# Attention value products on 64x64 tiles, upper and lower key halves in separate PSUM banks, in a hybrid encoder layer on one Trainium2 core

## The chip, the cores and the metric

The kernel runs on one core of a Trainium2 chip. The metric is the device time in microseconds (us). The engines are TensorE (PE in the profile, its weight loads PEld), VectorE (DVE), ScalarE (ACT), GpSimd (POOL) and SyncE (SP, which issues DMAs). SBUF is the on-chip memory, with 128 partitions; PSUM holds the results of matmuls, in banks of 128 partitions by 512 f32 numbers.

## The reference

One encoder layer with two parallel paths, over 4096 tokens of width 1024. The attention path has 8 query heads of 64 and 2 key-value heads, and a window of 128 tokens to each side, computed in blocks of 128 queries against 384 keys.

```python
o = jnp.einsum('bnkgqs,bnskd->bnqkgd', p.astype(v.dtype), vw)   # p: softmax with a sink, zero outside the window
...
a = banded_attention(q, k, v, rel_bias, attn_sink[l]) * jax.nn.silu(g_a)
p = multiscale_pool(u_p, pool_w[l], pool_scale[l]) * jax.nn.silu(g_p)
mixed = jnp.einsum('bse,ed->bsd', jnp.concatenate([a, p], axis=-1), w_out[l])
x = x + rmsnorm(mixed, post_norm_g[l])
```

The change concerns the first line, the product of attention weights and values, and the multiplication of its result by `silu(g_a)`, the gate.

## The kernel before

The program has two parts. Up to about 510 us it projects the gates and the pooled path and stores their results in DRAM. From there to the end it computes queries, keys and values, attention and the output product. Numbers are carried as pairs of f16 (a high part and the rest, "low"), so a product of two such numbers is three matmuls: high by high, low by high, high by low.

The second part goes through 32 blocks of 128 queries, from block 31 down to block 0. Two blocks are a unit `u`. For each block and each half of the head groups the steps are:

- `scores` (PE): queries by keys, on 64x32 tiles, into the score banks `s`.
- `logits` (DVE, L1336), four instructions: add the bias, take the maximum, write `p` to SBUF. The last one frees the score bank.
- `exps` (ACT, L1347), `denominators` (DVE), `probs` (ACT, L1369, the high part of the weights) and `rests` (DVE, L1377, the low part).
- `turn`: a DMA that transposes the weights into `pt`.
- `values` (PE, L1482), once for both halves: the value products. `vv` are the values, with keys on the partitions; the result has values on the partitions and queries along the free axis.
- `gate` (DVE, L1506): the result times the scale `gaf` and the gate `ga` (called `gb` in the trace), into `at`, 128x512 f32.

`gate` is followed by the output product in a form that saves matmuls: the four quarters of a pair of blocks are combined by sums (`sum1` L1567, `sum3` L1570 and `sum2` L1573 on DVE, `sum4` L1576 on POOL), each sum is cast to its high part (`high`, ACT L1534) and its low part (`low`, POOL or DVE L1538), and `product` (PE, L1632) multiplies each of the quarters and sums (named "11", "12", "22", "s1" to "s4") by a part of the output weights. `begin` (ACT L1650), `gain11` (DVE L1660), `gain` (L1666), `add` (DVE L1671) and `square` (ACT L1655) gather these products and norms from the PSUM banks `acc0`, `acc1` and `acc2`, and so free them. The same three banks hold the query, key and value projections (`aq`, `kv`, PE L1273 and L1414, kept by `keep_q` and the like with ACT L1262 and DVE L1263) and one half of the value products. The other half has a bank `o` of its own, with one buffer.

A block has the keys of three neighbouring blocks `kb` = 0, 1, 2. Besides `kb` 1, queries 0 to 63 of a block (`LOW`) see all of `kb` 0 and the lower half of `kb` 2; queries 64 to 127 (`TOP`) see all of `kb` 2 and the upper half of `kb` 0. Before, `LOW` queries accumulate in bank `o` and `TOP` queries in bank `p` (one of `acc`). Whole key blocks are taken with 128 keys on the partitions, as matmuls of 128x64 weights by 128 columns (two head groups in two column halves of the array). The edge halves (`kb` 2 for `LOW`, `kb` 0 for `TOP`) follow at the end on 64x64 tiles. An inner block has 72 matmuls and 72 weight loads. `gate` is two DVE instructions, one on each bank, each with half of the queries of all heads (128x256).

The order of all instructions is written out by hand: `due(t, fn, ...)` puts a step into a plan with a time, `pe(...)` does it for PE steps one behind the other, `at_` for steps at a time from a stretch's start `z`, `cast` for a pair of `high` and `low`, `soft` for a softmax. The plan is sorted by these times and each engine issues in that order; the engine then waits by semaphores. The head (blocks 31 to 28) and the tail (2 to 0) are tables of `at_` times. Between them a loop goes over the blocks from 27 down to 2, an odd and an even visit in one iteration of two blocks: an odd visit of block b has the value products and the gate of block b + 1 (even) and then `sums`; an even visit those of the odd block, and two query projections.

Of the kernel before, what the change touches and what calls it, by code (L numbers as in the profile page):

```python
# [8 lines left out]
F32 = mybir.dt.float32  # L9
# [3 lines left out]
AF = mybir.ActivationFunctionType  # L13
ALU = mybir.AluOpType
# [3 lines left out]
P = 128  # L18
# [5 lines left out]
NB = S // P  # L24
# [110 lines left out]
def hybrid_layer(ctx: ExitStack, tc, io, out):  # L135
    nc = tc.nc
# [25 lines left out]
    gaf = const.tile([P, 1], F32, name="gaf")  # L162
# [48 lines left out]
    with ExitStack() as actx:  # L211
# [13 lines left out]
        rows = pa.tile([P, T], F32, name="rows")  # L225
# [9 lines left out]
        def turn(name):  # L235
            turns[name] += 1
            return turns[name] % 2
# [377 lines left out]
        def pair(q, op, i, scale, key, group):  # L615
            src, r, w = raws[q][:, i], quarter_keys(q, i), f"w{slot[q, op]}"
            do("ACT", act(D) + 0.1, key, w_high, q, op, src, scale, r=r + [f"sw{group}"],
               w=[f"{w}h"])
            do("DVE", dve(D), key + 0.1, w_low, q, op, src, scale,
               r=r + [f"sw{group}", f"{w}h"], w=[f"{w}l"])  # L620
# [333 lines left out]
        b = turn("n2")  # L954
        for j in range(4):
            ld(9.5 + 0.1 * j, wut[:, j], io["w_uT"][j], 0.5, w=[f"wut{j}"])
            z = turn("sq")
            for half in range(2):
                t = U0 + 4 * j + 2 * half
# [245 lines left out]
        g = 0  # L1205
# [29 lines left out]
    pb = ctx.enter_context(tc.tile_pool(name="pb", bufs=2, reuse_waits="tile"))  # L1235
# [15 lines left out]
    q_t, v_t = {}, {}  # L1251
# [27 lines left out]
    pt, p_t, nm_t, den_t, rd_t, pn_t = {}, {}, {}, {}, {}, {}  # L1279

    def keys(b):
        return [kb for kb in range(3) if 0 <= b - 1 + kb < NB]
# [6 lines left out]
    def due(t, fn, *args):  # L1289
        plan.append((t, len(plan), fn, args))  # L1290
# [168 lines left out]
    ga_t, o_t = {}, {}  # L1459
# [5 lines left out]
    def values(b, bank):  # L1465
        kbs = keys(b)
        if bank is None:
            other = s_t[1][:, 0]
        else:
            other = gemm.tile([P, 512], F32, name=f"p{b}", tag=f"acc{bank}")  # L1470
        o_t[b] = [
            t[:, : 2 * P].rearrange("p (h j q) -> p h j q", h=2, j=2)
            for t in (ps_o.tile([P, 512], F32, name=f"o{b}", tag="o"), other)
        ]
        terms = ((0, 0), (1, 0), (0, 1))
        LOW, TOP = slice(0, P // 2), slice(P // 2, P)

        def part(half, kb, ks, side, vi, pi, start=False, stop=False):
            ku, kt = divmod(b - 1 + kb, 2)
            for g in range(2):  # L1480
                a = slice(64 * g, 64 * g + 64)
                nc.tensor.matmul(  # L1482
                    o_t[b][side][a, half], v_t[ku][ks, vi, kt, a],
                    pt[b, half][ks, pi, g, :, kb - kbs[0], (LOW, TOP)[side]],
                    start=start, stop=stop, skip_group_check=True,
                )

        for half in range(2):
            for kb, sides in ((1, (0, 1)), (0, (0,)), (2, (1,))):
                if kb in kbs:  # L1490
                    for n, (vi, pi) in enumerate(terms):
                        for side in sides:
                            part(half, kb, slice(0, P), side, vi, pi, start=(half == 0 and kb == 1 and n == 0))
        for half in range(2):
            for n, (vi, pi) in enumerate(terms):
                if 2 in kbs:
                    part(half, 2, LOW, 0, vi, pi, stop=(n == 2))
                if 0 in kbs:
                    part(half, 0, TOP, 1, vi, pi, stop=(n == 2))

    def gate(b):
        at[b] = pb.tile([P, 4, P], F32, name=f"at{b}", tag="at")
        o, ga = o_t.pop(b), ga_t.pop(b)
        for side in range(2):
            qs = slice(64 * side, 64 * side + 64)
            nc.vector.scalar_tensor_tensor(  # L1506
                out=at[b][:, :, qs], in0=o[side].rearrange("p h j q -> p (h j) q"), scalar=gaf,
                in1=ga[:, :, qs], op0=ALU.mult, op1=ALU.mult,
            )

    at, yf, y_t, mo_t, z_t, ss_t, xr_t, rs_t = {}, {}, {}, {}, {}, {}, {}, {}

# [63 lines left out]
    def sums(u, t):  # L1578
        due(t, sum1, u)
        due(t + 0.05, sum3, u)  # L1580
        due(t + 0.1, sum2, u)
        pair(t + 1.1, u, "s2", a11)
        pair(t + 10.0, u, "s3", a21)
        pair(t + 10.6, u, "s1", a_s1)
        due(t + 5.0, sum4, u)
        pair(t + 11.3, u, "s4", a12)
# [125 lines left out]
    def pe(us, fn, *args):  # L1712

        due(now[0], fn, *args)
        now[0] += us
        return now[0]
# [20 lines left out]

    def attend(b, bank):
        t = pe(2.0, values, b, bank)
        due(t, gate, b)  # L1740
        if b % 2:
            pair(t + 0.8, b // 2, "11", a11)
        else:
            sums(b // 2, t + 0.7)
# [51 lines left out]
    def at_(t, fn, *args):  # L1796
        due(z + t, fn, *args)
# [11 lines left out]
    def cast(th, tw, u, name, f, eng):  # L1809
        at_(th, high, u, name, f)  # L1810
        at_(tw, low, u, name, f, eng)
# [9 lines left out]
    for t, fn, *args in (  # L1821
# [13 lines left out]
        (32.6, scores, NB - 2, 1),  # L1835
        (33.7, proj_q1, U - 1, 1, 1, 1),
        (36.4, values, NB - 1, 0),
        (38.4, product, U, "22", OT4, 2),
        (41.0, scores, NB - 3, 0),
        (42.0, proj_k, U - 2, 1),  # L1840
        (44.7, proj_v, U - 2),
        (47.5, scores, NB - 3, 1),
        (48.4, product, U, "11", O11, 0),
        (51.1, values, NB - 2, 1),
        (53.1, product, U, "12", O21, 0, True),
        (55.7, scores, NB - 4, 0),
# [27 lines left out]
    cast(26.2, 27.0, U, "12", a12, G)  # L1874
    at_(33.9, keep_q, U - 1, 0)
    at_(38.35, keep_q, U - 1, 1)
    at_(38.37, gate, NB - 1)
    cast(41.0, 41.6, U, "11", a11, G)
    at_(46.3, keep_k, U - 2)
    at_(47.2, keep_v, U - 2)  # L1880
    at_(50.5, begin, U)
    at_(53.1, gate, NB - 2)
    at_(53.2, sum1, U)
    at_(54.1, sum3, U)
# [6 lines left out]
    at_(62.0, low_q, U - 2, 0)  # L1891
    at_(64.75, add, U, (0, HI), (0, HI), 0)
    cast(66.2, 66.8, U, "s3", a21, G)
    at_(66.75, gate, NB - 3)
    cast(66.8, 67.4, U, "s1", a_s1, G)
    cast(67.4, 68.0, U, "s4", a12, G)
# [35 lines left out]
    for b in reversed(range(2, NB - 4)):  # L1932
# [7 lines left out]
        if b % 2:  # L1940
            mix_p3(u + 2)
            do_kv(u - 1)
            attend(b + 1, int(b == NB - 5))
            visit(b, 1)
            mix_p4(u + 1)
            mix_p1(u + 1)
            mix_p6(u + 1)
            mix_p2(u + 1)
        else:
            do_q(u - 1, 0)  # L1950
            attend(b + 1, 0)
            visit(b, 1)
            do_q(u - 1, 1)
            due(now[0] + 2.1, load_x, u - 3)
            if b > 2:
                mix_p7(u + 1)
                mix_p5(u + 1)
# [54 lines left out]
    cast(5.8, 6.4, 1, "22", a22, G)  # L2012
    cast(6.4, 10.2, 1, "12", a12, G)
    at_(9.0, begin, 1)
    at_(13.7, gate, 2)
    at_(14.4, sum1, 1)
    at_(15.1, sum3, 1)
# [21 lines left out]

    cast(24.7, 26.1, 0, "22", a22, G)  # L2040
    cast(34.35, 35.0, 0, "12", a12, G)
    at_(33.9, gate, 1)
    cast(37.6, 38.6, 0, "11", a11, V)
    at_(45.9, gate, 0)
    cast(46.7, 47.3, 0, "21", a21, V)
    at_(30.0, open_unit, 0)
# [97 lines left out]
```

## Time and profile before

| | |
|---|---|
| median of 3 runs | 1164.87 us (1164.27 to 1165.51) |
| the profiled execution's own time | 1164.42 us |
| its span, first to last instruction | 1162.6 us |
| granted TensorE clock, mean | 1.000 |
| ACT busy | 701.7 us (60%), 1460 instructions |
| POOL busy | 314.4 us (27%), 310 instructions |

The profile shows one execution. "Busy" is the time in which an engine executes at least one instruction; register, branch, semaphore and DMA-issuing instructions don't count. A row of a timeline has the start in us from the span's start, the duration, the engine, the line of the kernel, the operation, output and inputs by name, the shape and a count; a bracket tells how long the engine was idle before it, and who ended this idle time. The timeline rolls neighbouring rows of one kind into one with a count. Ends of matmuls are modelled, so differences between starts are the better measure on PE.

### The profile page before, as it was taken

To read this page: it belongs to the slowest core of one execution; us is meant where nothing else is said; L and a number is where in the kernel's file an instruction comes from. 1 tells how busy PE (TensorE), PEld (TensorE's weight loads), DVE (VectorE), ACT (ScalarE), POOL (GpSimd) and SP (SyncE) were. 2 spreads that over 40 slices of the span, in tenths; PEclk is the share of its full clock that TensorE was granted. 3 is DMA by queue.
4 is the path that set the end of the run, shared out by engine and by line. 5 is a ranking of instruction groups with operands and counts; after the bars stand their busy time and mean duration, and the time that the engine had idled before them with its cause. 6 is when DMAs were issued, how large, how long until landed. Compare 5 with 4: busy or idle time off the path is not lost. (4 is left out here: it accounts for less than half of the span.)

```text
span 1162.6 us, 33001 instructions
## 1 busy us (share of the span) xinstructions
PE 1145.9 (99%) x13804; PEld 879.4 (76%) x13804; DVE 937.7 (81%) x1875; ACT 701.7 (60%) x1460; POOL 314.4 (27%) x310
## 2 busy tenths in 40 slices
PE   7999999999999999999999999999999999999997
PEld 6998888888888888986667676676666767667653
DVE  6889988988799973568878877887887887787786
ACT  6876546546654542267676676666666666666672
POOL 0001121211111010201534433533442443353231
PEclk9999999999999999999999999999999999999999
DMA  9645585867667664299886776886787678686784
GB/s 340 220 127 181 173 272 176 283 222 246 218 191 232 210 169 133 85 279 242 233 202 136 196 200 139 193 205 179 156 191 193 136 204 201 133 198 157 173 214 145
DMA packets 292981, 226.30 MB, mean 195 GB/s; under 512 B 210864, under 2 KB 250800, under 8 KB 288224
## 3 DMA queue, kind: packets, MB, share of 16 engines
q1 hardware_dynamic: 292832, 224.20, 69.8%
q8 instruction: 108, 1.77, 0.6%
q14 instruction: 41, 0.34, 0.1%
HBM read 114.68 MB, written 60.34 MB: 151 GB/s over the span
## 5 line engine op out<-in xcount | busy, mean ns | idle before, releaser
L689 PEld LDWEIGHTS <-wq 128*128 128x128 f16 x4104 | 400.9, 98 | 52.0 <-DVE wq L310 2.9
L689 PE MATMUL y<-xt,wq 128*128 128x256 f16 x1512 | 203.3, 273 | 0.1
L1347 ACT ACTIVATE p<-p,nm 128x385 f32<-128x385 f32 (+1 forms) x256 | 152.8, 599 | 36.5 <-POOL p L1330 20.4
L1273 PE MATMUL aq<-xb,xb 128*128 128x256 f16 x1024 | 173.4, 273 | 0.4 <-DVE mo L1671 0.4
L1632 PE MATMUL ms<-wo,ys 128*128 128x512 f16 x720 | 162.8, 379 | 0.3 <-DVE mo L1671 0.3
L1377 DVE SCALAR_TENSOR_TENSOR pn<-p,rd,pn 128x384 f16<-128x384 f32 (+1 forms) x256 | 158.3, 669 | 5.9 <-ACT pn L1369 5.9
L1336 DVE CUSTOM_DVE_ANT_0 p<-s,nt,nsink 128x384 f32<-128x384 f32 (+1 forms) x256 | 155.9, 666 | 2.0 <-PE s L1313 2.0
L1273 PEld LDWEIGHTS <-xb 128*128 128x128 f16 x1280 | 125.1, 98 | 23.4 <-issue 7.8
L1273 PE MATMUL aq<-xb,xt 128*128 128x256 f16 x512 | 139.6, 273 | 0.0
L1369 ACT ACTIVATE pn<-p,rd 128x384 f16<-128x384 f32 (+1 forms) x256 | 134.5, 596 | 4.0 <-issue 1.1
L307 POOL TENSOR_TENSOR yt<-yt,sg 128x512 f32<-128x512 f32 (+2 forms) x32 | 51.0, 1595 | 301.6 <-DVE yt L310 232.3
L1632 PEld LDWEIGHTS <-ys 128*128 128x128 f16 x720 | 69.2, 98 | 82.2 <-issue 3.8
L1632 PE MATMUL m<-wo,y 128*128 128x512 f16 x540 | 121.8, 379 | 0.0
L1632 PEld LDWEIGHTS <-y 128*128 128x128 f16 x540 | 51.4, 98 | 63.5 <-issue 3.6
L1666 POOL TENSOR_TENSOR mo<-mo,gpost 128x512 f32<-128x512 f32 x39 | 63.8, 1636 | 93.8 <-ACT jkb L1655 92.6
L689 PE MATMUL plain<-xb,wq 128*128 128x256 f16 x576 | 67.0, 273 | 3.7 <-DVE wq L310 2.3
L1273 PEld LDWEIGHTS <-xt 128*128 128x128 f16 x640 | 62.6, 98 | 8.7 <-issue 0.4
L689 PE MATMUL v<-xt,wq 128*128 128x256 f16 x504 | 68.6, 273 | 0.1
L689 PE MATMUL y<-xb,wq 128*128 128x256 f16 x504 | 68.6, 273 | 0.0
L689 PE MATMUL v<-xb,wq 128*128 128x256 f16 x504 | 68.6, 273 | 0.0
L689 PE MATMUL x<-xb,wq 128*128 128x256 f16 x504 | 68.1, 273 | 0.5 <-DVE ubuf L310 0.5
L1538 POOL TENSOR_TENSOR ys<-at,ys 128x512 f16<-128x512 f32 x29 | 38.5, 1326 | 93.3 <-ACT ys L1534 93.3
(218 smaller groups left out, 1935.4 us busy)
## 6 DMA issues: line engine op xcount, KB each, us to landing
nt<-in_xT SPq DMA_DIRECT2D x28, 512.0 KB
x_scr<-xb SPq DMA_DIRECT2D x14, 1024.0 KB
xb<-x_scr SPq DMA_DIRECT2D x14, 1024.0 KB
xr<-in_x SPq DMA_DIRECT2D x28, 512.0 KB
out<-xr SPq DMA_DIRECT2D x28, 512.0 KB
xn<-in_x SPq DMA_DIRECT2D x27, 512.0 KB
ga_scr<-cc SPq DMA_DIRECT2D x64, 128.0 KB
raw<-in_w_out SPq DMA_DIRECT2D x16, 512.0 KB
```

What stands on the lines that cost most here:

```text
L307: eng.tensor_tensor(out=out, in0=in0, in1=in1, op=op)
L689: nc.tensor.matmul(b[:, s], wq[:, slot[q, op], wv, s, k, :], x[:, xv, k, :], start=(first and k + s + wv + xv == 0), stop=(last and k == H ...
L1273: nc.tensor.matmul(acc, w[:, j, k, :], x[:, kh, v, kt, :], start=(n == 0), stop=(n == 3 * KT - 1),)
L1336: nc.vector.tensor_tensor_reduce(out=p_t[b, half][:, hh, :nk], in0=s_t[jj][:, gg, :nk], in1=bias[:, h, lo : lo + nk], scale=negc[:, h : h ...
L1347: nc.scalar.activation(p[:, hh, : nk + 1], p[:, hh, : nk + 1], AF.Exp, bias=nm_t[b, half][:, hh : hh + 1], scale=-1.0, accum_out=den_t[b, ...
L1369: nc.scalar.activation(prob_view(b, half)[:, 0, i], p_t[b, half][:, i, :nk], AF.Copy, scale=rd_t[b, half][:, i : i + 1],)
L1377: nc.vector.scalar_tensor_tensor(out=pn4[:, 1, i], in0=p_t[b, half][:, i, :nk], scalar=rd_t[b, half][:, i : i + 1], in1=pn4[:, 0, i], op0= ...
L1538: eng.tensor_tensor(out=y[:, :, 1], in0=f(u), in1=y[:, :, 0], op=ALU.subtract)
L1632: nc.tensor.matmul(z_t[u, tag], y[:, k, yi, :], wo[o][:, wi, k, :], start=(n == 0 and acc is None), stop=(n == 3 * HK - 1), skip_group_che ...
L1666: eng.tensor_tensor(out=mo, in0=mo, in1=gpost[:, cs], op=ALU.mult)
```

## The change

All value products use 64x64 tiles now. Each key block is cut into rows 0 to 63 and rows 64 to 127; the lower rows accumulate in bank `o`, the upper rows in bank `p`, each for all queries of the block (256 columns: two heads by 128 queries). Where the window cuts a half key block off (`kb` 0 with lower rows, `kb` 2 with upper rows), only the 64 queries that see it are taken (128 columns). A block still has 72 matmuls and 72 weight loads. As each bank now holds a part of the sum for all queries, the banks have to be added: a new step `copy_o` on ACT copies bank `o`, scaled, to `at`; `gate` is a DVE instruction that adds the scaled bank `p`, and a second one that multiplies by the gate, both 128x512. ACT gets 32 instructions more, DVE's count stays; the order on POOL and SP and that of all DMAs is as before. The new lines behind `gate` are two numbers lower (L1534 is L1532, L1632 is L1630).

```diff
-        for half in range(2):
-            for kb, sides in ((1, (0, 1)), (0, (0,)), (2, (1,))):
-                if kb in kbs:
-                    for n, (vi, pi) in enumerate(terms):
-                        for side in sides:
-                            part(half, kb, slice(0, P), side, vi, pi, start=(half == 0 and kb == 1 and n == 0))
-        for half in range(2):
-            for n, (vi, pi) in enumerate(terms):
-                if 2 in kbs:
-                    part(half, 2, LOW, 0, vi, pi, stop=(n == 2))
-                if 0 in kbs:
-                    part(half, 0, TOP, 1, vi, pi, stop=(n == 2))
+        order = [kb for kb in (1, 0, 2) if kb in kbs]
+        for half in range(2):
+            for kb in order:
+                for n, (vi, pi) in enumerate(((0, 0), (1, 0), (0, 1))):
+                    for rows in range(2):
+                        qs = {(0, 0): LOW, (2, 1): TOP}.get((kb, rows), slice(0, P))
+                        part(half, kb, rows, qs, vi, pi, ...)
+
+    def copy_o(b):
+        at[b] = pb.tile([P, 4, P], F32, name=f"at{b}", tag="at")
+        nc.scalar.activation(
+            at[b], o_t[b][0].rearrange("p h j q -> p (h j) q"), AF.Copy, scale=gaf
+        )
 
     def gate(b):
-        at[b] = pb.tile([P, 4, P], F32, name=f"at{b}", tag="at")
-        o, ga = o_t.pop(b), ga_t.pop(b)
-        for side in range(2):
-            qs = slice(64 * side, 64 * side + 64)
-            nc.vector.scalar_tensor_tensor(
-                out=at[b][:, :, qs], in0=o[side].rearrange("p h j q -> p (h j) q"), scalar=gaf,
-                in1=ga[:, :, qs], op0=ALU.mult, op1=ALU.mult,
-            )
+        nc.vector.scalar_tensor_tensor(
+            out=at[b], in0=o_t.pop(b)[1].rearrange("p h j q -> p (h j) q"), scalar=gaf,
+            in1=at[b], op0=ALU.mult, op1=ALU.add,
+        )
+        nc.vector.tensor_tensor(out=at[b], in0=at[b], in1=ga_t.pop(b), op=ALU.mult)
...
     def attend(b, bank):
         t = pe(2.0, values, b, bank)
+        due(t - 0.3, copy_o, b)
         due(t, gate, b)
...
+    at_(38.07, copy_o, NB - 1)
     at_(38.37, gate, NB - 1)
...
+    at_(52.80, copy_o, NB - 2)
     at_(53.1, gate, NB - 2)
...
+    at_(13.40, copy_o, 2)
     at_(13.7, gate, 2)
```

The copies of blocks 29, 1 and 0 stand in the tables in the same way, 0.3 ahead of their gates.

The order of PE in an inner block of the loop (block 22), at the place where key block 0 follows key block 1. Before, the rows are (`o`: queries `LOW`; the tile has 128 keys):

```order
L1482 LDWEIGHTS vv_8638
L1482 MATMUL p_10149<-pt_0_9844,vv_8638 64x128
L1482 LDWEIGHTS vv_9431
L1482 MATMUL o_10150<-pt_0_9844,vv_9431 64x128
L1482 LDWEIGHTS vv_9431
L1482 MATMUL o_10150<-pt_0_9844,vv_9431 64x128
```

The same place of the changed kernel (`o`: lower rows of the keys, `p`: upper rows; 64 keys on each tile):

```order
L1482 LDWEIGHTS vv_8643
L1482 MATMUL p_10158<-pt_0_9853,vv_8643 64x256
L1482 LDWEIGHTS vv_9438
L1482 MATMUL o_10159<-pt_0_9853,vv_9438 64x2x64
L1482 LDWEIGHTS vv_9438
L1482 MATMUL o_10159<-pt_0_9853,vv_9438 64x2x64
L1482 LDWEIGHTS vv_9438
L1482 MATMUL p_10158<-pt_0_9853,vv_9438 64x256
L1482 LDWEIGHTS vv_9438
L1482 MATMUL p_10158<-pt_0_9853,vv_9438 64x256
```

Where one bank was filled alone with 128 columns at a time, the two banks now alternate, with 128 columns on one and 256 on the other.

DVE in the loop at the gate of the same block (`k_all` and `vv` are the low parts of keys and values, `yf` a quarter of the pooled path). Before:

```order
L1263 SCALAR_TENSOR_TENSOR k_all<-kv_10042,k_all 128x256
L1263 SCALAR_TENSOR_TENSOR vv_10224<-kv_10042,vv_10224 128x256
L1506 SCALAR_TENSOR_TENSOR at_10229<-o_10150,gaf,gb_9908 128x4x64
L1506 SCALAR_TENSOR_TENSOR at_10229<-p_10149,gaf,gb_9908 128x4x64
L1567 TENSOR_TENSOR s_11_10280<-at_10229,yf_11_9579 128x512
```

Now:

```order
L1263 SCALAR_TENSOR_TENSOR k_all<-kv_10051,k_all 128x256
L1263 SCALAR_TENSOR_TENSOR vv_10233<-kv_10051,vv_10233 128x256
L1505 SCALAR_TENSOR_TENSOR at_10238<-p_10158,gaf,at_10238 128x512
L1509 TENSOR_TENSOR at_10238<-at_10238,gb_9917 128x512
L1565 TENSOR_TENSOR s_11_10290<-at_10238,yf_11_9587 128x512
```

The gate's place is the same; both of its instructions are twice as wide, and the first reads what ACT wrote.

ACT in the head, around the gates of blocks 31 and 30 (`p`, `nm` are those of the softmax, `q` and `aq` a query projection, `y` a cast quarter). Before:

```order
L1347 ACTIVATE p_1_6740,den_1_6738<-p_1_6740,nm_1_6737 128x385 x4
L1262 ACTIVATE q_1_6807<-aq_1_6626 128x512
L1369 ACTIVATE pn_1_6826<-p_1_6740,rd_1_6739 128x384 x4
L1534 CAST y_15_6882<-at_6810 128x4x128
L1347 ACTIVATE p_0_6917,den_0_6915<-p_0_6917,nm_0_6914 128x385 x4
```

Now, up to the second gate:

```order
L1347 ACTIVATE p_1_6740,den_1_6738<-p_1_6740,nm_1_6737 128x385 x4
L1500 ACTIVATE at_6805<-o_6754,gaf 128x512
L1262 ACTIVATE q_1_6809<-aq_1_6626 128x512
L1369 ACTIVATE pn_1_6827<-p_1_6740,rd_1_6739 128x384 x4
L1532 CAST y_15_6883<-at_6805 128x4x128
L1347 ACTIVATE p_0_6918,den_0_6916<-p_0_6918,nm_0_6915 128x385 x4
L1262 ACTIVATE k_all<-kv_6890 128x256
L1369 ACTIVATE pn_0_6980<-p_0_6918,rd_0_6917 128x384 x2
L1262 ACTIVATE vv_6984<-kv_6890 128x256
L1369 ACTIVATE pn_0_6980<-p_0_6918,rd_0_6917 128x384 x2
L1648 COPY mo_0_7063<-m_15_7039 128x512
L1347 ACTIVATE p_1_7060,den_1_7058<-p_1_7060,nm_1_7057 128x385 x4
```

The copy of block 31 stands between the four exps and the copy of the query projection; that of block 30 is the next row, behind the last four exps here and ahead of the following weights (`pn`).

More of the change, by code (lines that the diff above doesn't have):

```diff
@@ L1471, in values, with part @@
         o_t[b] = [
-            t[:, : 2 * P].rearrange("p (h j q) -> p h j q", h=2, j=2)
+            t.rearrange("p (h j q) -> p h j q", h=2, j=2)
             for t in (ps_o.tile([P, 512], F32, name=f"o{b}", tag="o"), other)
         ]
-        terms = ((0, 0), (1, 0), (0, 1))
         LOW, TOP = slice(0, P // 2), slice(P // 2, P)
-        def part(half, kb, ks, side, vi, pi, start=False, stop=False):
+        def part(half, kb, rows, qs, vi, pi, start, stop):
             ku, kt = divmod(b - 1 + kb, 2)
+            ks = (LOW, TOP)[rows]
             for g in range(2):
@@ L1482, in part @@
                 nc.tensor.matmul(
-                    o_t[b][side][a, half], v_t[ku][ks, vi, kt, a],
-                    pt[b, half][ks, pi, g, :, kb - kbs[0], (LOW, TOP)[side]],
+                    o_t[b][rows][a, half, :, qs], v_t[ku][ks, vi, kt, a],
+                    pt[b, half][ks, pi, g, :, kb - kbs[0], qs],
                     start=start, stop=stop, skip_group_check=True,
                 )
+        order = [kb for kb in (1, 0, 2) if kb in kbs]
         for half in range(2):
-            for kb, sides in ((1, (0, 1)), (0, (0,)), (2, (1,))):
-                if kb in kbs:
-                    for n, (vi, pi) in enumerate(terms):
-                        for side in sides:
-                            part(half, kb, slice(0, P), side, vi, pi, start=(half == 0 and kb == 1 and n == 0))
@@ L1494, in values @@
-        for half in range(2):
-            for n, (vi, pi) in enumerate(terms):
-                if 2 in kbs:
-                    part(half, 2, LOW, 0, vi, pi, stop=(n == 2))
-                if 0 in kbs:
-                    part(half, 0, TOP, 1, vi, pi, stop=(n == 2))
-    def gate(b):
-        at[b] = pb.tile([P, 4, P], F32, name=f"at{b}", tag="at")
-        o, ga = o_t.pop(b), ga_t.pop(b)
-        for side in range(2):
-            qs = slice(64 * side, 64 * side + 64)
-            nc.vector.scalar_tensor_tensor(
-                out=at[b][:, :, qs], in0=o[side].rearrange("p h j q -> p (h j) q"), scalar=gaf,
-                in1=ga[:, :, qs], op0=ALU.mult, op1=ALU.mult,
-            )
+            for kb in order:
+                for n, (vi, pi) in enumerate(((0, 0), (1, 0), (0, 1))):
+                    for rows in range(2):
+                        qs = {(0, 0): LOW, (2, 1): TOP}.get((kb, rows), slice(0, P))
+                        part(half, kb, rows, qs, vi, pi,
+                             start=(half == 0 and kb == 1 and n == 0),
+                             stop=(kb == order[-1] and n == 2))
@@ L1893, in hybrid_layer @@
     cast(66.2, 66.8, U, "s3", a21, G)
+    at_(66.45, copy_o, NB - 3)
     at_(66.75, gate, NB - 3)
@@ L2041, in hybrid_layer @@
     cast(34.35, 35.0, 0, "12", a12, G)
+    at_(33.60, copy_o, 1)
     at_(33.9, gate, 1)
     cast(37.6, 38.6, 0, "11", a11, V)
+    at_(45.60, copy_o, 0)
     at_(45.9, gate, 0)
```

## The prediction

> **What bounds the kernel now.** I read the page's busy shares first, then what PE (TensorE) waited for in the attention and output stage (520 us to the end), then that stage's timelines, engine by engine, around each gate.
>
> ```profile
> PE 1145.9 (99%) x13804; PEld 879.4 (76%) x13804; DVE 937.7 (81%) x1875; ACT 701.7 (60%) x1460; POOL 314.4 (27%) x310
> ```
> ```profile
> PE o L1482 <- DMA pt<-pn: 0.8, 1, 0.8
> PE z L1604 <- DVE xb L1671: 0.6, 1, 0.6
> PE aq L1273 <- DVE mo L1671: 0.4, 2, 0.3
> PE ms L1632 <- DVE mo L1671: 0.3, 1, 0.3
> ```
>
> PE is busy 99% of the span, and in this whole stage it waits 2.1 us for others (the columns: total, times, longest). So a nanosecond saved on PE is a nanosecond off the end, but only while no chain that feeds PE (gate, sums, cast, low half, weights) grows past its slack. The change touches both: the products are the gain, the gate is the price.
>
> **The products.** The timeline of PE in a steady block; columns are start, duration, engine, line, operation, operands, tile, shape, count.
>
> ```profile
> 711.12 0.27 PE L1273 MATMUL aq<-xb,xt 128*128 128x256 f16 x1
> 711.23 0.38 PE L1273 MATMUL aq<-xb,xb 128*128 128x256 f16 x2
> ...
> 716.02 0.25 PE L1482 MATMUL o<-pt,vv 128*64 128x128 f16 x2
> 716.10 0.22 PE L1482 MATMUL p<-pt,vv 128*64 128x128 f16 x2
> 716.15 0.22 PE L1482 MATMUL o<-pt,vv 128*64 128x128 f16 x2
> ...
> 717.48 0.24 PE L1482 MATMUL o<-pt,vv 64*64 64x128 f16 x2
> ...
> 717.94 0.93 PE L1313 MATMUL s<-k_all,q 64*32 64x288 f16 x48
> ```
>
> A block takes 717.94 - 716.02 = 1.92 us. Starts 0.11 us apart are the price of 256 columns, starts 0.055 apart that of 128. The 24 steps of 0.055 up to 717.48 are 1.34 of 1.46, so a change of tile shape costs about 0.1. From 717.48 six steps on 64x64 tiles, upper and lower keys side by side, and the next change fill 0.46. After, each of the four array tiles has per block 12 matmuls of 256 columns and 6 of 128: 12 x 0.11 + 6 x 0.055 = 1.65, and 0.13 for turnover: 1.78. If the tiles run independently, this saves 0.14 in each of 30 inner blocks and, by the same count, 0.12 in each of the two edge blocks: **4.4 us**, were PE the only thing.
>
> Independence is what has to hold, because the two row tiles get unequal widths (128 against 256) wherever the window cuts. No value product of before shows that. The scores of block 0 do: 48 matmuls on 8 tiles, six rounds, with 160 columns on some tiles and 192, 224 or 256 on their neighbours.
>
> ```profile
> 1118.41 0.85 PE L1313 MATMUL s<-k_all,q 64*32 64x160 f16 x48
> ```
>
> The groups by shape in the stretch from 1119.05 to 1119.30 (busy, mean ns, idle):
>
> ```profile
> L1313 PE MATMUL s<-k_all,q 64*32 64x256 f16 x4 | 0.4, 269 | 0.0
> L1313 PE MATMUL s<-k_all,q 64*32 64x224 f16 x4 | 0.4, 256 | 0.0
> L1313 PE MATMUL s<-k_all,q 64*32 64x192 f16 x2 | 0.2, 243 | 0.0
> ```
>
> No 160 is left there while the 256s still run: narrow tiles had worked through their rounds ahead of the wide ones. In lockstep, or with all starts in program order, the last 160 would belong to the last round. I take independent tiles. The Trainium skill, "TensorE: Matmul & The Clock Gate", section "Part 3: Packing small matmuls — row/col tiling", states that matmuls start and end strictly in program order. The rows just quoted disagree with that for neighbouring tiles, and by it the sum would be that of the third rival below.
>
> **Prices of the new gate.** A gate of before in the steady loop, on DVE (VectorE), with the sum behind it:
>
> ```profile
> 698.63 0.47 DVE L1506 SCALAR_TENSOR_TENSOR at<-o,gaf,gb 128x256 f32<-128x256 f32 x1
> 699.02 0.48 DVE L1506 SCALAR_TENSOR_TENSOR at<-p,gaf,gb 128x256 f32<-128x256 f32 x1
> 699.53 1.17 DVE L1567 TENSOR_TENSOR s<-at,yf 128x512 f32<-128x512 f32 x1
> ```
>
> The nearest rows for the new operations, an ACT (ScalarE) read of a 128x512 PSUM bank, a DVE operation on two SBUF operands, and one on PSUM and SBUF:
>
> ```profile
> 523.85 0.57 ACT L1262 ACTIVATE q<-aq 128x512 f16<-128x512 f32 x1
> ```
> ```profile
> 539.28 0.69 DVE L1567 TENSOR_TENSOR s<-at,yf 128x512 f32<-128x512 f32 x1
> ...
> 545.08 0.69 DVE L1660 TENSOR_TENSOR mo<-m,gpost 128x512 f32<-128x512 f32 x1 [1.27 <-ACT jkb L1655]
> ```
>
> So: the copy 0.57 to 0.62, taken as 0.6; the add from PSUM 0.69; the multiply 0.69 where nothing holds it. Back to back such instructions start 0.6 apart, the old halves 0.39 apart. Before, a gate kept DVE 0.78; now 1.2, behind a copy of 0.6 that DVE must wait for: 0.4 to 0.5 more on DVE and up to 1.0 more delay.
>
> One price has no row. The multiply reads two SBUF operands like sum1, which at 699.53 took 1.17 instead of 0.69 while POOL (GpSimd) was at work:
>
> ```profile
> 697.88 2.27 POOL L1538 TENSOR_TENSOR y<-yf,y 128x512 f16<-128x512 f32 x2
> ```
>
> POOL ended at 700.15, and sum1 at 700.70, half a microsecond behind it; the old gate, which reads PSUM and one SBUF operand, kept its 0.47 in the same stretch. The multiply in that place thus lasts between 0.69 (not held) and until 700.70 (held). I take held, by the row of the same operation on the same kinds of operands.
>
> **The steady loop: -1.3 us.** What follows the gate in an odd visit:
>
> ```profile
> 702.19 0.62 ACT L1534 CAST ys<-at 128x512 f16<-128x512 f32 x1 [3.94 <-DVE at L1573]
> ```
> ```profile
> 702.89 1.16 POOL L1538 TENSOR_TENSOR ys<-at,ys 128x512 f16<-128x512 f32 x1 [2.13 <-ACT ys L1534]
> ```
> ```profile
> 704.54 0.81 PE L1632 MATMUL ms<-wo,ys 128*128 128x512 f16 x3
> ```
>
> The copy starts when PE is done, about 698.5, on an ACT that idles until 702.19 (3.94 of idle): until 699.1. The add runs to 699.8, the multiply to 700.70 as held, and sum1 from there, now free of POOL, to 701.43 where it ended at 700.70: +0.73. sum3, sum2, the cast (702.19) and POOL's low half (702.89) move along. The low half landed at 704.05, and PE's third matmul from 704.54, the first that needs it, comes at about 704.76: slack 0.71. PE itself now arrives 0.14 earlier or not at all, so 0.15 to 0.23 becomes a stall. In even visits DVE is busy with the rests of the softmax when the copy runs, so the copy is hidden, and 0.5 more on DVE is taken up by its gaps ahead of the next query copies. An iteration of two blocks saves 0.28 and gives back 0.18: -0.1, times 13.
>
> **The head, blocks 31 to 29: +3.8 us.** Three times a bank that PE wants is freed behind a gate.
>
> ```profile
> 525.85 3.10 DVE L1377 SCALAR_TENSOR_TENSOR pn<-p,rd,pn 128x384 f16<-128x384 f32 x4
> ```
> ```profile
> 530.86 1.10 PE L1313 MATMUL s<-k_all,q 64*32 64x288 f16 x48
> ...
> 546.31 2.75 PE L1632 MATMUL ms<-wo,ys 128*128 128x512 f16 x12
> ```
> ```profile
> 538.57 0.60 ACT L1347 ACTIVATE p<-p,nm 128x385 f32<-128x385 f32 x1
> ```
>
> 1. The copy of block 31 stands between the last exp and the query copy of 523.85 on ACT. The query copy, its low half on DVE and the gate slip by 0.55, and the gate is 0.5 longer: the rests start at 526.9 instead of 525.85, and the logits behind them slip as much. These free the bank of the scores at 530.86, which wait already (1.10 instead of 0.93 at 717.94): PE +1.1. The 0.8 that PE waits for pt gives 0.3 back.
> 2. The copy of block 30 stands behind the exp that ends at 539.17, itself 1.06 later: it ends at 540.8, and add and multiply at about 542.2. sum1 starts there instead of at 539.28: +2.9. In order behind the waiting add on DVE are the denominators and rests of block 29 and the gain of 545.08, which frees the bank of the product at 546.31: 0.54 of slack (545.77 to 546.31). PE +2.4.
> 3. The add of L1671 behind it frees the next query bank. The waits list shows PE waiting for that line already, so no slack: PE +3.0. The third gate, block 29, adds about 0.8 in the same way. The 0.4 that three blocks save is inside these arrival times.
>
> **The tail, blocks 2 to 0: +2.2 us.**
>
> ```profile
> 1112.59 0.63 ACT L1655 ACTIVATE jkb<-mo 128x512 bf16<-128x512 f32 x1 [1.60 <-DVE mo L1671]
> ```
> ```profile
> 1113.02 0.48 DVE L1506 SCALAR_TENSOR_TENSOR at<-o,gaf,gb 128x256 f32<-128x256 f32 x1
> ...
> 1117.90 0.68 DVE L1336 CUSTOM_DVE_ANT_0 p<-s,nt,nsink 128x384 f32<-128x384 f32 x1
> ```
> ```profile
> 1138.87 1.46 PE L1604 MATMUL z<-wo,xt 128*128 128x512 f16 x6 [0.61 <-DVE xb L1671]
> ```
>
> The copy of block 2 stands behind the square of 1112.59 and ends at 1113.9, so the gate starts 0.9 later than 1113.02 and is 0.5 longer: +1.4 on DVE. The logits end at 1118.58 and free the bank of the second half of the scores of 1118.41, at about 1118.66: slack 0.08. PE +1.5. Blocks 1 and 0 each put up to 0.5 more on the DVE chain for which PE waits at 1138.87: an estimated +0.9. Less 0.2 to 0.3 for the shorter blocks: +2.2.
>
> **Sum.** 1164.42 us of the profiled execution + 3.8 - 1.3 + 2.2 = **1169.1**. That execution lies 0.45 below the median 1164.87, inside the spread of the runs; from the median it would be 1169.6. POOL's and SP's instructions and all DMA issues stand in the order of before, and cost nothing of their own.
>
> **Rivals.** *Absorbed (faster).* The chains of head and tail have slack that I don't see, and PE, 99% busy, keeps its 4.4: 1160.0. For it: DVE is 81% busy and has gaps to catch up. Against it: the 1.10 of the scores at 530.86. It decides at the logits before these: it holds if they slip by under 0.1 and the chain of s2 by under 0.71. *Not held (no difference).* POOL doesn't hold the multiply: it ends 0.3 earlier, sum1 with it, no stall in the loop, -3.6 there, and a little less in the head: 1166. For it: nothing shows this very instruction. Against it: sum1's 1.17. *Starts in order (slower).* The narrow matmuls wait for their wide neighbour's start: a block is 1.87, 0.09 less saved in each of 30, half of it taken from the stalls: 1164.42 + 4.7 + 1.3 = 1170.4. Against it: the shapes in the scores of block 0. *Lockstep, so that the change doesn't shorten the products.* 18 rounds of 0.11 and turnover are 2.1, 0.33 above my block, 30 times: 1178.9. The same rows speak against it.
>
> **How the numbers follow.** Forecast 0.58 (its own range 1167 to 1173: the copy at 0.57 to 0.66, the stall at 0 to 0.3, half a microsecond at each of the steps of head and tail), not held 0.18, absorbed 0.13, in order 0.07, lockstep 0.04. No difference is within 0.2%, 2.3 us, about what a measurement of this kernel can tell from none: 1162.5 to 1167.2. Faster 0.13 (absorbed); same 0.22 (not held, and 0.04 from the forecast's lower edge); slower 0.65. The range 1164.0 to 1173.0 leaves out absorbed and lockstep.
>
> **What would show it.** From the first value product to the next scores 1.77 to 1.80 us (1.87: in order; 2.1: lockstep). The new multiply in odd visits about 0.9 or more (0.69: not held). PE waiting 0.15 to 0.23 for s2's weights in the 13 iterations. The logits of block 29 a microsecond late, PE 3 to 4 us behind the old trace by 569, about 2.5 by the end of the loop, and 4 to 5 at the end. If the scores at 530.86 haven't moved, the forecast is wrong at its first step.

## The result, and the profile after

The changed kernel takes 1171.09 us (median of 4 runs, 1169.78 to 1172.15) against 1164.73 before in the same comparison (1164.27 to 1165.51): a ratio of 1.0054, with a 95% interval of 1.0042 to 1.0067. It is slower by 6.4 us. The profiled execution took 1171.33 us, with a span of 1169.5. One execution of all that follow, 4173.10 us of the kernel under "The place of the copy", is left out of that kernel's numbers.

The busy shares on the page, and what TensorE (PE) waited for in the attention and output stage (total, times, longest):

```profile
PE 1144.8 (98%) x13804; PEld 876.6 (75%) x13804; DVE 952.0 (81%) x1875; ACT 721.6 (62%) x1492; POOL 315.3 (27%) x310
```
```profile
PE z L1602 <- DVE xb L1669: 2.1, 1, 2.1
PE o L1482 <- DMA pt<-pn: 2.1, 5, 0.7
PE ms L1630 <- DVE mo L1658: 1.7, 1, 1.7
PE s L1313 <- DVE nm L1336: 1.5, 3, 0.7
PE aq L1273 <- DVE mo L1669: 0.5, 1, 0.5
PE ms L1630 <- DVE mo L1669: 0.5, 1, 0.5
PE ms L1630 <- DVE q L1263: 0.5, 1, 0.5
PE z L1602 <- DVE at L1505: 0.5, 1, 0.5
PE kv L1273 <- DVE q L1263: 0.4, 1, 0.4
```

The waits add up to 9.8 us, where before there were 2.1. Where they lie is seen by comparing the start of the same matmuls in the two traces (before; after less before):

| PE's work | starts before | later by |
|---|---|---|
| values of block 31 | 520.32 | 0.11 |
| product behind the scores of 530.86 | 531.88 | 1.31 |
| product "s2", head | 546.31 | 2.93 |
| query projection, head | 552.01 | 3.41 |
| value projection, end of the head | 568.97 | 4.19 |
| query projection, end of the loop | 1093.60 | 1.81 |
| scores behind the values of block 2 | 1112.27 | 2.41 |
| product behind the first scores of block 0 | 1119.19 | 3.31 |
| last products (L1604), second group | 1135.51 | 3.89 |
| last products, the group that waits | 1138.87 | 5.42 |
| values of block 0 | 1144.14 | 7.04 |

So the head loses 4.1 us, the loop gains 2.4, and the tail loses 5.1.

**The products.** PE in the block that was shown before (start, duration, engine, line, operation, operands, tile, shape, count):

```profile
719.82 0.30 PE L1482 MATMUL o<-pt,vv 64*64 64x256 f16 x2
...
720.23 0.28 PE L1482 MATMUL o<-pt,vv 64*64 64x128 f16 x4
720.28 0.27 PE L1482 MATMUL p<-pt,vv 64*64 64x256 f16 x2
720.34 0.27 PE L1482 MATMUL o<-pt,vv 64*64 64x256 f16 x2
720.39 0.27 PE L1482 MATMUL p<-pt,vv 64*64 64x256 f16 x2
...
721.59 0.93 PE L1313 MATMUL s<-k_all,q 64*32 64x288 f16 x48
```

The block is 1.77 us long instead of 1.92. Bank `o` begins its next key block (720.34) before bank `p` begins the last matmul of the old one (720.39), which stands ahead of it in the program: the row tiles do run independently. By the rule of the Trainium skill ("TensorE: Matmul & The Clock Gate", "Part 3: Packing small matmuls — row/col tiling"), with all starts in program order, the block would have been 1.87; these rows disagree with it for neighbouring tiles.

**A gate in the loop.** Timelines of ACT, DVE and POOL at the gate of the same block of the loop that was shown before:

```profile
702.37 0.69 ACT L1500 ACTIVATE at<-o,gaf 128x512 f32<-128x512 f32 x1 [0.19 <-PE p L1482]
```
```profile
703.09 0.75 DVE L1505 SCALAR_TENSOR_TENSOR at<-p,gaf,at 128x512 f32<-128x512 f32 x1 [0.45 <-ACT at L1500]
703.88 0.76 DVE L1509 TENSOR_TENSOR at<-at,gb 128x512 f32<-128x512 f32 x1
704.67 0.69 DVE L1565 TENSOR_TENSOR s<-at,yf 128x512 f32<-128x512 f32 x1
```
```profile
701.81 2.28 POOL L1536 TENSOR_TENSOR y<-yf,y 128x512 f16<-128x512 f32 x2
```

The copy takes 0.69 us and the add 0.75. By the time that the multiply starts, POOL has 0.2 left, so the multiply is hardly held. `sum1` ends 4.66 later than the 700.70 of before, 0.89 behind a PE that is 3.77 later here. The weight loads (PEld) of product "s2" and its matmuls show what becomes of it:

```profile
708.10 0.31 PEld L1630 LDWEIGHTS <-ys 128*128 128x128 f16 x2
708.76 0.33 PEld L1630 LDWEIGHTS <-ys 128*128 128x128 f16 x3 [0.34 <-POOL ys L1536]
```
```profile
708.32 1.05 PE L1630 MATMUL ms<-wo,ys 128*128 128x512 f16 x4
```

The two loads of the first row are 0.21 apart, so the third, the first of the low half, was due at 708.53 and comes 0.23 late, at 708.76. The first matmul starts at 708.32, when the second load does: each load here starts one matmul of 0.21 us ahead of its use. The third matmul, due at 708.74, therefore starts only about 0.02 later, at 708.76, and those behind it are 0.03 later.

**The head.** The second gate, on ACT and DVE, and PE's longest wait in the head, behind it:

```profile
540.48 0.67 ACT L1500 ACTIVATE at<-o,gaf 128x512 f32<-128x512 f32 x1
```
```profile
541.18 0.75 DVE L1505 SCALAR_TENSOR_TENSOR at<-p,gaf,at 128x512 f32<-128x512 f32 x1 [1.40 <-ACT at L1500]
541.97 0.69 DVE L1509 TENSOR_TENSOR at<-at,gb 128x512 f32<-128x512 f32 x1
542.70 0.69 DVE L1565 TENSOR_TENSOR s<-at,yf 128x512 f32<-128x512 f32 x1
```
```profile
549.24 2.75 PE L1630 MATMUL ms<-wo,ys 128*128 128x512 f16 x12 [1.73 <-DVE mo L1658]
```

DVE stands idle for 1.40 us for the copy, which stood behind the exps, and `sum1` starts at 542.70 instead of 539.28.

**The tail.** The gate of block 1, and what it does to PE (the first and third rows are the third and fourth exps of block 0):

```profile
1137.35 0.49 ACT L1347 ACTIVATE p<-p,nm 128x257 f32<-128x257 f32 x1
1137.84 0.67 ACT L1500 ACTIVATE at<-o,gaf 128x512 f32<-128x512 f32 x1
1138.41 0.49 ACT L1347 ACTIVATE p<-p,nm 128x257 f32<-128x257 f32 x1
```
```profile
1138.59 0.75 DVE L1505 SCALAR_TENSOR_TENSOR at<-p,gaf,at 128x512 f32<-128x512 f32 x1 [0.95 <-issue]
1139.38 0.69 DVE L1509 TENSOR_TENSOR at<-at,gb 128x512 f32<-128x512 f32 x1
1139.99 1.13 DVE L1354 TENSOR_SCALAR den<-den 128x4 f32<-128x4 f32 x1
```
```profile
1139.58 1.50 POOL L1536 TENSOR_TENSOR xt<-yf,xt 128x512 f16<-128x512 f32 x1 [9.22 <-ACT xt L1532]
```
```profile
1144.29 4.37 PE L1602 MATMUL z<-wo,xt 128*128 128x512 f16 x12 [2.14 <-DVE xb L1669]
```

The same instruction and the same matmuls before:

```profile
1135.04 0.17 DVE L1354 TENSOR_SCALAR den<-den 128x4 f32<-128x4 f32 x1
```
```profile
1138.87 2.75 PE L1604 MATMUL z<-wo,xt 128*128 128x512 f16 x12 [0.61 <-DVE xb L1671]
```

DVE idles 0.95 until the copy is done. Then a tiny instruction on 128x4 numbers takes 1.13 us, until POOL's operation ends at 1141.08; before, it took 0.17. PE waits 2.14 us at the end of this chain (before: 0.61), and its next 12 matmuls take 4.37 (before: 2.75). The last goes with the clock, by the table of 1 us stretches (busy us of PE, PEld, DVE, ACT and POOL with counts, then the granted TensorE clock, the DMA share and GB/s):

```profile
1144.00:1145.00 1.00, 0.71 (x2) 0.25 (x2) 1.00 (x2) 0.72 (x2) 0.00 (x0) 0.59 0.08 15
1145.00:1146.00 1.00, 1.00 (x4) 0.34 (x3) 1.00 (x3) 0.00 (x0) 0.00 (x0) 0.50 1.15 213
1146.00:1147.00 1.00, 1.00 (x4) 0.39 (x3) 0.96 (x3) 0.00 (x0) 0.00 (x0) 0.50 1.18 216
1147.00:1148.00 1.00, 1.00 (x5) 0.34 (x3) 1.00 (x2) 0.00 (x0) 0.00 (x0) 0.70 1.12 363
1148.00:1149.00 1.00, 1.00 (x7) 0.46 (x5) 1.00 (x4) 0.00 (x0) 0.78 (x1) 1.00 0.78 315
```

After the idle stretch the clock is 0.50 to 0.70 for some 3 us, which costs 1.6 us: 5.42 to 7.04 in the table of shifts. This is one execution; whether the other three of the changed kernel had it is not shown.

### The profile page after: what moved, and what is told of

It reads as the page before. It is cut to its first block, busy times and chain, and to the rows that moved or that the text cites. A ratio compares the mean times of both kernels' runs of the same rounds, so it can differ in the third digit from the quotient of the medians.

```text
span 1169.5 us, 33065 instructions
## 1 busy us (share of the span) xinstructions
PE 1144.8 (98%) x13804; PEld 876.6 (75%) x13804; DVE 952.0 (81%) x1875; ACT 721.6 (62%) x1492; POOL 315.3 (27%) x310
## 3 DMA queue, kind: packets, MB, share of 16 engines
q8 instruction: 108, 1.77, 0.6%
## 5 line engine op out<-in xcount | busy, mean ns | idle before, releaser
L1630 PE MATMUL ms<-wo,ys 128*128 128x512 f16 x720 | 163.4, 379 | 2.7 <-DVE mo L1658 1.7
L1630 PEld LDWEIGHTS <-ys 128*128 128x128 f16 x720 | 68.1, 98 | 86.4 <-issue 6.0
L1630 PE MATMUL m<-wo,y 128*128 128x512 f16 x540 | 121.8, 379 | 0.0
L1630 PEld LDWEIGHTS <-y 128*128 128x128 f16 x540 | 51.4, 98 | 63.6 <-ACT at L1500 3.1
```

The lines of the kernel that those rows point to most:

```text
L1630: nc.tensor.matmul(z_t[u, tag], y[:, k, yi, :], wo[o][:, wi, k, :], start=(n == 0 and acc is None), stop=(n == 3 * HK - 1), skip_group_che ...
```

## The experiments

Theory A: the products gain what their blocks show, and everything lost is the chain of copy, add and multiply, in head and tail first of all through the place of the copy on ACT. The rivals: the products' gain is not there at the end (B); the loop pays as much as head and tail (C); the width of the two DVE instructions costs, and the copy's place doesn't matter (A2). Medians are compared with that of the kernel before in the same series: 1164.89 us for the products alone, the gate alone, the loop alone and the early copies, 1165.15 for the other four.

### Products and gate apart

The first keeps the new products and takes the old gate, each half of it on one bank, so that half of each sum is left out:

```diff
-    def copy_o(b): ...
     def gate(b):
+        for side in range(2):
+            qs = slice(64 * side, 64 * side + 64)
+            nc.vector.scalar_tensor_tensor(
+                out=at[b][:, :, qs], in0=o[side].rearrange("p h j q -> p (h j) q")[:, :, qs],
+                scalar=gaf, in1=ga[:, :, qs], op0=ALU.mult, op1=ALU.mult)
```

> The new products alone: all value products on 64x64 tiles as in the change, but no copy, and the gate in its old form and cost (two VectorE instructions of 128x256); it reads queries 0 to 63 from bank o and 64 to 127 from bank p, so the other half of each sum is left out. Theory A (the products gain what their blocks show, the loss is all in the chain copy, add, multiply): 30 x 0.15 + 2 x 0.13 us less than before, 1160.0 us, between 1159.5 and 1161, with no new wait of TensorE. Rival B (the products' gain is handed back at other waits, or the products cost something that the block's length doesn't show): 1163 or more.

Measured: 1160.87 us, 4.0 less, ratio 0.9963 (0.9950 to 0.9977). The blocks are as short as in the change (4.8 in all). In the profile 0.7 of that comes back at PE's waits (2.8 where before there were 2.1), at two places:

```profile
PE aq L1273 <- DVE mo L1666: 0.9, 2, 0.5
PE z L1599 <- DVE xb L1666: 0.8, 1, 0.8
```

Before, these two were 0.4 and 0.6: PE comes earlier to places that had no slack. Rival B falls, but the expected "no new wait" was too simple.

The second keeps the old products and takes the new gate, whose copy and add read the 256 numbers of each bank twice:

```diff
+    def wide(t):
+        return t.rearrange("p h j q -> p (h j q)").unsqueeze(1).to_broadcast([P, 2, 256])
...
-            at[b], o_t[b][0].rearrange("p h j q -> p (h j) q"), AF.Copy, scale=gaf
+            at[b].rearrange(...), wide(o_t[b][0]), AF.Copy, scale=gaf
```

> The new gate alone: products as before the change, but with copy, add and multiply, each 512 wide (both banks hold 256 numbers a partition, which the copy and the add read twice, so the output is not the layer's). Theory A: what the change loses plus what its products gain, 6.4 + 4.8 = 11 us above before, 1175.8, between 1173 and 1178. Rival B (the loss comes with the products): 1165 to 1169.

Measured: 1174.68 us, 9.8 more, ratio 1.0084 (1.0070 to 1.0098). The two parts, -4.0 and +9.8, make 5.8 of the change's 6.4. The gate is the whole of the loss.

### Head, loop and tail apart

In these three the old and the new form stand side by side, and the block's number decides (each kernel has one of the returns):

```diff
+    def NEW(b):
+        return 2 < b < NB - 3            # the loop alone
+        return b < NB - 3                # all but the head
+        return 2 < b < NB - 3 and b % 2  # odd blocks of the loop
```

> The change in blocks 28 to 3 alone (the loop); blocks 31 to 29 and 2 to 0 as before the change. Theory A (head and tail lose, the loop gains): 26 x 0.15 = 3.9 us gained, 0.03 x 13 = 0.4 lost at the weights of s2, 0.9 to 1.2 lost at three late transposed weights: 1162.2 us, between 1161.2 and 1163. Rival C (the wider gate costs as much in the loop, hidden in the trace by an execution's scatter): 1165 or more.

Measured: 1162.71 us, 2.2 less than before, ratio 0.9980 (0.9971 to 0.9988), over 11 runs. Rival C falls: the loop gains. This is the lowest median here of a kernel that computes the whole layer. In the loop (560 to 1100 us) PE waits 0.8 for late transposed weights, which before it did not:

```profile
PE o L1524 <- DMA pt<-pn: 0.8, 3, 0.3
PE ms L1686 <- DVE mo L1725: 0.3, 1, 0.3
```

> The change without its head: blocks 31 to 29 as before the change, 28 to 0 as changed. Theory A: the head's loss of 4.1 us goes, its products' 0.4 are already inside that: loop -2.4 and tail +5.1 remain, 1167.4 us, between 1166 and 1168.5. Rival (the head's delay is absorbed later, so taking it away doesn't move the end): 1170 to 1171.

Measured: 1167.34 us, 2.2 more, ratio 1.0018 (1.0009 to 1.0027). Against the change's 6.4, the head's 4.2 us are gone at the end, as the shifts say: nothing absorbs them.

> The change in the 13 odd blocks 27 to 3 alone; the even blocks of the loop, whose gate is followed by the sums, the head and the tail as before the change. Theory A (the loop's losses, late weights of s2 and late transposed weights, come from the even blocks' gate, behind which the sums and then the logits stand): 13 x 0.15 = 2.0 us gained and nothing lost: 1162.9 us, waits of TensorE in the loop as before. Rival (the transposed weights are late because of the odd blocks' gate): 1163.8 to 1164.2, with three waits of 0.3 to 0.4 in the loop.

Measured: 1163.14 us, 2.0 less, ratio 0.9982 (0.9973 to 0.9991), and in the loop the transposed weights are in time again:

```profile
PE ms L1686 <- DVE mo L1725: 0.3, 1, 0.3
```

So the late weights come with the even blocks; that it is through the logits, which stand behind the gate and the sums, is argued, not shown. The products of the 13 even blocks are shorter by the same 2.0, but the medians with and without them differ by only 0.2 to 0.4 us, which is within their intervals: that the even blocks gain anything at the end is not shown.

### The place of the copy

```diff
-    at_(38.07, copy_o, NB - 1)
-    at_(38.37, gate, NB - 1)
+    at_(36.45, copy_o, NB - 1)
+    at_(36.5, gate, NB - 1)
...
-    at_(52.80, copy_o, NB - 2)
+    at_(51.5, copy_o, NB - 2)
...
-    at_(13.40, copy_o, 2)
+    at_(12.2, copy_o, 2)
...
-    at_(33.60, copy_o, 1)
+    at_(32.2, copy_o, 1)
```

> The change with the copies of blocks 31, 30, 2 and 1 earlier on ScalarE (ahead of exps or of the square that they stood behind), and the gate of block 31 ahead of the query copy's low half. Theory A1 (in head and tail it is the copy's place that costs, more than the width of the two VectorE instructions): block 1 gives back 1.5 to 2 us of TensorE's wait at the first product of unit 0 and with it the 1.6 us of the reduced clock, block 2 0.8, blocks 31 and 30 about 2 together: 1165.5 us, between 1164 and 1167.5. Rival A2 (the width costs, the place doesn't matter): 1170 to 1171.

Measured: 1166.08 us (10 runs), 1.2 above before, ratio 1.0009 (1.0000 to 1.0018). Five numbers give back 5.0 to 5.2 us of the change's loss, with the width of the instructions as it was: A2 falls. The products' 4.0 and the remaining 1.2 say that some 5.2 us of the gate's price, half of it, are left, in its width, the copy itself, and the waits that it still causes; no run here tells these apart. The clock is 1.00 in the tail here until PE's last matmul.

The last of these numbers alone:

```diff
-    at_(33.60, copy_o, 1)
+    at_(32.2, copy_o, 1)
```

> The change with the copy of block 1 alone moved ahead of the four exps of block 0 on ScalarE. Theory A1 (the copy's place): the gate ends about 1 us earlier, the small VectorE instruction behind it is no longer held by GpSimd (1 us), TensorE's wait of 2.1 us falls to 0.3 to 0.6, and its clock is not reduced after it (1.6 us in the profiled execution): 1168.2 us, between 1167.5 and 1169.6. Rival A2 (the two wide VectorE instructions cost, not the place): 1170.5 to 1171.3.

Measured: 1168.36 us, 3.2 more than before, ratio 1.0024 (1.0012 to 1.0035): this one number gives back half of the change's 6.4. DVE and PE at that place:

```profile
1137.65 0.75 DVE L1505 SCALAR_TENSOR_TENSOR at<-p,gaf,at 128x512 f32<-128x512 f32 x1
1138.44 0.69 DVE L1509 TENSOR_TENSOR at<-at,gb 128x512 f32<-128x512 f32 x1
1139.06 0.17 DVE L1354 TENSOR_SCALAR den<-den 128x4 f32<-128x4 f32 x1
```
```profile
1142.90 2.75 PE L1602 MATMUL z<-wo,xt 128*128 128x512 f16 x12 [1.28 <-DVE xb L1669]
```

The gate starts 0.94 earlier and the tiny instruction takes 0.17 again. PE's wait is 1.28 instead of 2.14, more than the 0.3 to 0.6 expected, and 12 matmuls take 2.75.

### The tiny instruction behind the gate

```diff
-    cast(34.35, 35.0, 0, "12", a12, G)
+    cast(31.9, 32.0, 0, "12", a12, G)
```

> The change with one cast of the tail (quarter 12 of unit 0, ScalarE and then GpSimd) ahead of block 0's exps instead of behind them, so that GpSimd's operation is over before the gate of block 1. If GpSimd held the 128x4 VectorE instruction behind that gate (1.13 instead of 0.17 us), it is short now, TensorE's wait of 2.1 us falls to about 1.2, and the reduced clock after it may go with it: 1170.1, or 1168.5 where the clock stays. If something else held it: 1171.

Measured: 1169.20 us, 4.1 more than before, ratio 1.0036 (1.0022 to 1.0050): 2.3 of the change's 6.4 are gone. POOL is through before the gate, the instruction takes 0.16, and PE waits 1.18 instead of 2.14:

```profile
1141.27 0.16 DVE L1354 TENSOR_SCALAR den<-den 128x4 f32<-128x4 f32 x1
```
```profile
1144.61 2.75 PE L1602 MATMUL z<-wo,xt 128*128 128x512 f16 x12 [1.18 <-DVE xb L1669]
```

So it was POOL's operation that held it, for 1 us of PE's wait, and the clock is not reduced after the shorter wait. In the two other kernels that have the late copy at this place (the new gate alone and the one without the new head) the instruction takes 1.12 and ends with POOL's operation too.

## Why the prediction was right, and where its sum was not

The direction and the range held: 1169.1 forecast, 1171.1 measured. By its steps, in the profiled execution:

- **Products, 0.14 a block:** 0.15 measured, 4.8 in all instead of 4.4, of which 4.0 arrive at the end when they stand alone. Both rivals on the order of the tiles (1.87 and 2.1 us a block) are out by the block's 1.77.
- **Head, +3.8:** +4.1. Step by step, PE is 1.2, 2.8 and 3.3 later where 1.1, 2.4 and 3.0 were worked out, and `sum1` starts at 542.7 where 542.2 was. The mechanism is the one named, the copy behind the exps; the copy (0.67 for 0.6) and the add (0.75 for 0.69) were a little too cheap. The rival "absorbed" falls at the place named for it, the scores of 530.86, whose second half waits 0.64 for the logits.
- **Loop, -1.3:** -2.4, and two errors in it cancel in part. The stall at the weights of s2 is 0.03, not 0.15 to 0.23. The chain is about as late as forecast and more (0.89 for 0.73), so it is the slack that was mis-sized: it was counted to 704.76, when the load of the weights is due, but the third matmul from 704.54 starts two steps of 0.21 later, at 704.97. On this point the rival "not held" came out right, for another reason: the copy and the add are slow enough for POOL to be nearly done when the multiply starts. What the step left out are the transposed weights: three blocks of the loop (27, 17 and 7) wait for them and take 2.15 to 2.34 instead of 1.77, 1.4 more in all. A wait of 0.3 of before, at 836 us, is gone. 3.9 of shorter blocks, less 0.4 at s2 and 1.4 at those three, and 0.3 for the wait, is 2.4.
- **Tail, +2.2:** +5.1, the step that failed. Block 2 cost 1.5 as worked out (1.81 to 3.31 by the shifts): its copy ends at 1115.79, behind the square, and DVE's lateness grows from 1.90 to 3.42 by the logits. PE spends 0.6 of that earlier than forecast, waiting for block 2's transposed weights, and the rest at the scores. For blocks 1 and 0 an "estimated +0.9" stood there, taken from the width of the gate, where the rows of ACT would have shown that block 1's copy stands behind three exps. It was 3.6: the copy's place and, following from it in this execution, the instruction held by POOL (1.0) and the clock after the wait (1.6), less the shorter blocks. The copy's place alone gave 3.2 back. The hold and the clock had no row before the change.

The errors of the three sums, +0.3, -1.1 and +2.9, make 2.1 of the 2.2 us by which the profiled execution lies above the forecast. That the forecast came this near is in part luck: the loop's error hides a third of the tail's, and most of the tail's loss had causes that the prediction did not name.

## What to carry to other kernels

Work that is moved to a less busy engine stands in that engine's order: what it costs is the end of whatever is ahead of it there, plus a handover, and not its own duration. Find out at every place where it is issued, and not for a typical one, what that is; moving four copies and one gate ahead of their neighbours was worth about 5 us here, more than the 4.0 that the new products gain. A change whose gain is per block and whose price is at the edges can be made in the middle alone, as in the kernel of 1162.7 us.

## What the hardware showed unexpectedly

- An idle stretch of 2.14 us on PE was followed by a clock of 0.50 and 12 matmuls in 4.37 us instead of 2.75. The profile of the kernel without the new head shows it twice, in the tail and in the head:

```profile
1142.95 4.44 PE L1658 MATMUL z<-wo,xt 128*128 128x512 f16 x12 [2.13 <-DVE xb L1725]
```
```profile
537.54 0.25 PE L1485 MATMUL o<-pt,vv 128*64 128x128 f16 x2 [1.75 <-DMA pt<-pn]
538.79 4.45 PE L1686 MATMUL m<-wo,y 128*128 128x512 f16 x12
```

  That execution took 1170.07 us, the longest of its ten. The length of the idle time does not decide alone: the kernel with the new gate alone has 2.13 us at the same place and no reduced clock. Of the nine idle stretches of 1.6 to 2.2 us in the attention and output stages of all ten profiles, three were followed by it; after the four of 1.1 to 1.4 us the clock stayed at 1.00. What decides was not tried.
- In the program's first part, between 12 and 25 us, the profiles of all eight experiments have a stretch of 3 to 7 us at such a reduced clock as well; those of the kernel before and of the change don't. The values of block 31 start 0.0 to 1.4 us later in them than before, so the ends of the experiments' profiles are not compared here, only their medians.
- A DVE instruction on 128x4 numbers, with one SBUF operand, was held for 1 us by POOL, and POOL's operation took 1.50 instead of 1.15. The Trainium skill, "SBUF — State Buffer", section "Who interferes with whom", states that such a scaling instruction can take the ports that DVE shares with GpSimd, and then waits for the whole of the other's instruction; the row of 1139.99, which ends 0.04 us after POOL, agrees.
- PE's wait for the transposed weights of block 30 is 0.8 us before the change and 1.8 in two kernels with the same code there (the one without the new head and the odd blocks alone). So that microsecond doesn't come from the change; it is most likely scatter from one execution to the next, and where PE waits for a DMA, single profiles can't be compared more closely than that.
